# Gated values of the first chunk begun in an earlier memory unit, their casts one step later, residual rows loaded two blocks ahead

## The chip, the cores and the metric

The kernel runs on one core of a Trainium2 chip. A core has TensorE (PE in the profile, with its weight loads apart as PEld), VectorE (DVE), ScalarE (ACT), GpSimd (POOL) and SyncE (SP, here the one queue from which every DMA is issued). The metric is the device time of one execution in microseconds; lower is better.

## The reference

One decoder layer on 2048 tokens of width 1024, in fp32. With this depth its mixer is the dilated sliding-window attention; four memory heads attend to 256 memory tokens.

```python
h = rmsnorm(x, norm_g[i])
proj = h @ w_in[i]                       # q | k | v | memory q | gate
mix = dilated_window_mixer(q, k, v)      # 3 groups of 4 heads; groups weighted by their softmax denominators
mo = memory_attention(qm, rmsnorm(mem, mem_norm_g[i]), w_mem_kv[i])
y = jnp.concatenate([mix, mo], axis=-1) * jax.nn.silu(gate)
x = x + y @ w_out[i]
return rmsnorm(x, final_norm_g)
```

## The kernel before, in words

Every fp32 product of the projections is made of three fp32r matrix multiplications: an operand is split into a rounded high part and the rest (xH, xL for the values, wh, wl for the weights), and high x high, low x high and high x low are added up in one PSUM bank (L140 to L142, and L665 to L667 in the output stage).

The work goes in order of units. Six pairs of sequence heads come first, four chunks of 512 tokens each. Then come eight memory units (the loop at L806), each with a query projection, a gate projection and the attention of two memory heads over one chunk. The output stage follows (`out_block`, L650): 16 blocks of 128 tokens, four to a chunk c, each with two banks of 512 columns (three in the last), and each bank with eight values of k times three multiplications, called a chain of 24 here. There are three PSUM banks of this kind, so a chain can begin when the bank of the chain three earlier has been read. The reader is the residual addition (L670), which adds the row of x to the bank; a square sum, a root and a scaling with g_fin follow, and the row is stored (L687).

A unit's attention has parts that drag on behind it. Score steps (L451 on PE) fill banks; ACT takes the exponentials (L460) into one of four buffers p; POOL divides by the sums (L467); DVE transposes 32 x 32 blocks (L329), SP stores them to a DRAM buffer t_dr (L332) and loads them back turned (L338); a value step (L440, eight small multiplications for one half of a unit) then reads that p. Two halves fill one bank, and DVE multiplies it by the gate u (L420, the gate product). A p buffer is given to a new softmax when the value step that read it is done. The nine value steps from 773.69 us on are numbered 1 to 9 in what follows.

A gated value (`make_y`, L617) of chunk c and index k (128 of the 1024 columns, as many as one k of a chain needs) goes back from DRAM: z_dr holds the gated product and f_dr the group weights of the sequence heads. SP issues z and, for k below 6, two loads of f; after two steps z and f are multiplied (the weighing or product, L634, on POOL for k of 1 and 4, on DVE else); after three ACT casts the high part (L635); after four DVE makes the rest (L636). Four buffers for z and three for f go round.

The program is written with delays: `at(d, fn)` puts fn d steps later, and a step is a part of a projection or of a block; a unit and a block have eight steps. A scheduler then sets each engine's order of instructions from dependences and its own cost estimates. At run time every engine takes its instructions strictly in that order, and so does SP with the DMAs: an instruction that waits holds up those behind it.

The lines that the change touches: `make_y` and its staging buffers (L615 to L636), the loading of a residual row (L657, called in `out_block`), and the two loops that place these steps (L811 to L815, and L822 to L824).

Of the kernel before, what the change touches and what calls it, by code (L numbers as in the profile page):

```python
# [9 lines left out]
F32 = mybir.dt.float32  # L10
F32R = mybir.dt.float32r
AF = mybir.ActivationFunctionType
ALU = mybir.AluOpType
# [4 lines left out]
P = 128  # L18
# [3 lines left out]
CH = 512  # L22
# [12 lines left out]
def trunk_kernel(ctx, tc, xT, xrows, w_in, g_in, w_out, memT, mrows, g_mem, w_mem, g_fin, nbias, ident_in, out):  # L35
    nc = tc.nc
    v, a, pe, gp, sp = nc.vector, nc.scalar, nc.tensor, nc.gpsimd, nc.sync
# [9 lines left out]
    Rb = const.tile([P, S], F32, name="Rb")  # L47
# [19 lines left out]
    def sb(shape, dt, tag, bufs):  # L67
        return pool.tile(shape, dt, tag=tag, name=f"{tag}_{nc.next_id()}", bufs=bufs)
# [4 lines left out]
    def pbank(p=ps_p, tag="pp"):  # L73
        return p.tile([P, CH], F32, tag=tag, name=f"{tag}_{nc.next_id()}")
# [32 lines left out]
    def r_view(g, c):  # L107
        if g == 0:
            return Rb.rearrange("p (r c n) -> p r c n", r=16, c=4)[:, :, c, :]
        if g == 1:  # L110
            return Rb.rearrange("p (j r n) -> p j r n", j=4, r=4)[:, :, c, :]
        return Rb[:, c * CH:(c + 1) * CH]
# [31 lines left out]
    def proj_mm(ps, w, g, c):  # L144
        for k in range(NK):
            proj_k_mm(ps, w, g, c, k)
            if k % 2 and k < NK - 1:
                yield
# [98 lines left out]
    def scaled(dst, ps, g, c):  # L247

        v.tensor_tensor(to_blocks(dst, g), from_proj(ps, g), r_blocks(g, c), op=ALU.mult)  # L249
# [32 lines left out]
    def proj_q(st, g, c, w, ps=None):  # L282
        if ps is None:
            ps = pbank()
            yield from proj_mm(ps, w, g, c)
        q = sb([P, CH], F32, "q", 2)
        if g == 3:
            v.scalar_tensor_tensor(q, ps, SCALE, r_view(g, c), op0=ALU.mult, op1=ALU.mult)
        else:
            scaled(q, ps, g, c)  # L290
        st["q"] = q
        yield
# [322 lines left out]
    staged = []  # L615

    def make_y(c, k):  # L617

        yH, yL = xH[:, 2 + c % 2, k, :], xL[:, 2 + c % 2, k, :]
        cs = slice(c * CH, (c + 1) * CH)  # L620
        if not staged:
            kk = sb([P, 5 * P], F32, "kk", 2)
            vb = sb([P, 5, P], F32, "vb", 2).rearrange("p b n -> p (b n)")
            staged.append([Rb[:, i * CH:(i + 1) * CH] for i in range(3)] + [vb[:, :CH]])
            staged.append([sb([P, CH], F32, "wraw", 2), sb([P, CH], F32, "wraw", 2), kk[:, :CH]])
        t, f = staged[0][k % 4], staged[1][k % 3]
        sp.dma_start(t, z_dr[k // 2][:, k % 2, cs])
        if k < 6:
            for h in range(2):
                sp.dma_start(f[h * HD:(h + 1) * HD, :],  # L630
                             f_dr[k // 2, 2 * (k % 2) + h:2 * (k % 2) + h + 1, cs].broadcast_to([HD, CH]))

        if k < 6:
            at(2, lambda: (gp if k in (1, 4) else v).tensor_tensor(t, t, f, op=ALU.mult))  # L634
        at(3, lambda: a.copy(yH, t))  # L635
        at(4, lambda: v.tensor_tensor(yL, t, yH.bitcast(F32), op=ALU.subtract))  # L636

    outr = out.rearrange("(u r) d -> r u d", r=16)
    gfin = []
# [2 lines left out]
    def load_rows(r):  # L642
        residual[r] = row_tile("wh")
        sp.dma_start(residual[r], xr[r])
# [5 lines left out]
    def out_block(c, b):  # L650
        yH, yL = xH[:, 2 + c % 2], xL[:, 2 + c % 2]
        r = 4 * c + b
        bs = slice(b * P, (b + 1) * P)
        x_t = residual.pop(r)
        last = r == 15
        if not last:
            at(3, lambda: load_rows(r + 1))  # L657
        cuts = (0, 512, 768, 1024) if last else (0, 512, 1024)
        ss = sb([P, 6], F32, "ss", 2)
        sq = row_tile("wl")  # L660
        for i, (lo, hi) in enumerate(zip(cuts, cuts[1:])):
            ns = slice(lo, hi)
            ps = pbank()[:, :hi - lo]
            for k in range(NK):
                pe.matmul(ps, yH[:, k, bs], woH[:, k, ns], start=(k == 0), stop=False)  # L665
                pe.matmul(ps, yH[:, k, bs], woL[:, k, ns], start=False, stop=False)  # L666
                pe.matmul(ps, yL[:, k, bs], woH[:, k, ns], start=False, stop=(k == NK - 1))  # L667
                if k % 2:
                    yield
            v.tensor_tensor(x_t[:, ns], ps, x_t[:, ns], op=ALU.add)  # L670
            if last:
                a.activation(sq[:, ns], x_t[:, ns], AF.Square, accum_out=ss[:, 3 + i:4 + i])
                if i == 0:
                    v.tensor_tensor(x_t[:, ns], x_t[:, ns], gfin[0][:, ns], op=ALU.mult)
        if last:
            v.tensor_reduce(ss[:, 0:1], ss[:, 3:6], axis=AX.X, op=ALU.add)
        else:
            a.activation(sq, x_t, AF.Square, accum_out=ss[:, 0:1])
        rsqrt_mean(ss[:, 1:2], ss[:, 0:1], ss[:, 2:3], ss[:, 3:4])
        if last:  # L680
            a.activation(x_t[:, :CH], x_t[:, :CH], AF.Copy, scale=ss[:, 1:2])
            v.scalar_tensor_tensor(x_t[:, CH:], x_t[:, CH:], ss[:, 1:2], gfin[0][:, CH:], op0=ALU.mult, op1=ALU.mult)
            for n in range(2):
                sp.dma_start(outr[r][:, n * CH:(n + 1) * CH], x_t[:, n * CH:(n + 1) * CH])
        else:
            v.scalar_tensor_tensor(x_t, x_t, ss[:, 1:2], gfin[0], op0=ALU.mult, op1=ALU.mult)
            at(2, lambda: sp.dma_start(outr[r], x_t))  # L687
# [11 lines left out]
    def at(delay, fn):  # L699
        todo.setdefault(slot[0] + delay, []).append(fn)  # L700

    def run(gen):
        for _ in gen:
            for fn in todo.pop(slot[0], []):
                fn()
            slot[0] += 1
# [39 lines left out]
    for idx, (g, pp) in enumerate(pairs):  # L746
# [21 lines left out]
        if idx < 5:  # L768
            n = 2 * pairs[idx + 1][0] + pairs[idx + 1][1]
# [36 lines left out]
    for n, (pp, c) in enumerate(((0, 0), (0, 1), (1, 0), (1, 1), (0, 2), (1, 2), (0, 3), (1, 3))):  # L806
        st = {}
        if n == 3:
            for i in range(2 * NK):
                at(4 * i // 3, lambda i=i: load_wo(i))  # L810
        elif n == 6:  # L811
            for k in range(NK):
                at(2 * k, lambda k=k: make_y(0, k))
        elif n == 7:
            at(3, lambda: load_rows(0))  # L815
            at(5, load_gfin)
        run(proj_q(st, 3, c, ws[2 + 2 * pp]))
        run(proj_gate(st, 3, c, ws[1 + 2 * pp], "nb" if n % 3 == 1 else "u"))
        burst((st, 3, pp, c), 2)
    for c in range(NC):  # L820
        for b in range(4):
            if c < NC - 1:  # L822
                for i in range(2):
                    at(1 + 3 * i, lambda k=2 * b + i: make_y(c + 1, k))  # L824
            run(out_block(c, b))
            if c == 0 and b in (0, 2):
                burst()
# [62 lines left out]
```

## Time and profile before

| | |
|---|---|
| median of 3 runs | 999.66 us (999.1 to 1000.13) |
| profiled execution | 999.68 us |
| its span | 997.6 us |
| PE busy | 964.0 us (97%) |
| DVE busy | 428.0 us (43%) |
| ACT busy | 325.6 us (33%) |
| POOL busy | 244.3 us (24%) |
| mean granted clock of TensorE | 0.982 |

The span runs from the first to the last instruction of the profiled execution. PEclk, the granted clock, is a share of 2.4 GHz. A row of the timeline gives the start in us from the span's start, how long the instruction took, the engine, the line, the operation, output and inputs, and in brackets the idle time of the engine before it and what ended that. Matmul rows overlap: the time from one start to the next is what one costs. Line numbers are those of the kernel before; in the changed kernel the same code stands two or three lines further down (weighing L636, cast L637, rest L638, row load L646, chains L667 to L669, residual addition L672, store L689).

### The profile page before, as it was taken

The page shows a single profiled execution, that of the slowest core. Times are in us where ns is not written, and L with a number is a line of the kernel's source. Part 1 is how long each engine was busy: PE and PEld are TensorE (multiplying, and loading weights), DVE is VectorE, ACT ScalarE, POOL GpSimd, SP SyncE. Part 2 cuts the span into 40 slices and gives each one's busy share as a digit, 9 for nine tenths or more (in the row PEclk, how much of TensorE's full clock was granted, in tenths as well). Part 3 has the DMA queues.
Part 4 walks back from the last instruction along what each step waited for, and adds up shares of the span by engine and source line. Part 5 has one row for each costly group of instructions (what it writes and reads, how often), then busy time and mean ns, then how long its engine had stood idle before and what let it go on. Part 6 is the DMA issues. An engine that isn't in the chain of part 4 may idle for free.

```text
span 997.6 us, 13866 instructions
## 1 busy us (share of the span) xinstructions
PE 964.0 (97%) x4836; PEld 757.9 (76%) x4836; DVE 428.0 (43%) x995; ACT 325.6 (33%) x992; POOL 244.3 (24%) x391
## 2 busy tenths in 40 slices
PE   8899999999999999999999999999999788999997
PEld 5688888887788887877777777787777466788886
DVE  7867333333333333333334334335543544465333
ACT  5756432242223222332233232433232330232111
POOL 4411500050004100321123011245356450011000
PEclk9899999999999999999999999999999889899999
DMA  5455321141224322442345432534465876877311
GB/s 196 156 190 190 127 75 53 54 144 67 76 86 133 124 82 85 129 136 85 95 117 157 121 92 85 174 134 129 117 213 172 219 224 182 272 242 234 127 64 63
DMA packets 102133, 135.17 MB, mean 136 GB/s; under 512 B 29872, under 2 KB 63920, under 8 KB 102064
## 3 DMA queue, kind: packets, MB, share of 16 engines
q1 hardware_dynamic: 102064, 134.30, 42.9%
q8 instruction: 38, 0.62, 0.3%
q14 instruction: 31, 0.25, 0.1%
HBM read 89.14 MB, written 45.12 MB: 135 GB/s over the span
## 4 chain that ended last, share of the span: by engine, by line
PE 86%; DMA 3%; DVE 3%; issue 3%; POOL 2%; ACT 1%; SPq 1%; POOLq 0%; ACTq 0%; DVEq 0%
PE pp L140 20%; PE pp L142 19%; PE pp L141 19%; PE pp L665 6%; PE pp L666 6%; PE pp L667 6%; PE ps L395 4%; PE po L417 3%; PE ps L451 1%; PE po L440 1%; DMA wraw<-in_w_in 1%; POOL p L467 1%; POOL wl L78 1%; DMA wl<-in_g_fin 1%; DMA wh<-in_xrows 1%
## 5 line engine op out<-in xcount | busy, mean ns | idle before, releaser
L140 PE MATMUL pp<-xH,wh 128*128 128x512 f32 x896 | 360.9, 403 | 3.0 <-DVE kk L249 2.9
L142 PE MATMUL pp<-xH,wl 128*128 128x512 f32 x896 | 356.9, 398 | 1.8 <-DVE wl L78 1.8
L141 PE MATMUL pp<-xL,wh 128*128 128x512 f32 x896 | 356.9, 398 | 1.4 <-DVE xL L198 1.4
L140 PEld LDWEIGHTS pp<-xH,wh 128*128 128x128 f32 x896 | 169.5, 189 | 51.6 <-issue 7.7
L142 PEld LDWEIGHTS pp<-xH,wl 128*128 128x128 f32 x896 | 169.2, 189 | 46.0 <-DVE wl L78 3.6
L141 PEld LDWEIGHTS pp<-xL,wh 128*128 128x128 f32 x896 | 169.5, 189 | 42.8 <-DVE xL L198 2.7
L320 POOL COPY vb<-mid 32x128 f32<-32x128 f32 (+1 forms) x208 | 59.4, 285 | 248.5 <-DVE mid L317 240.3
L665 PE MATMUL pp<-xH 128*128 128x512 f32 (+1 forms) x264 | 105.3, 399 | 12.0 <-ACT xH L635 6.6
L320 ACT COPY vb<-mid 32x128 f32<-32x128 f32 (+1 forms) x208 | 60.7, 292 | 167.4 <-DVE mid L317 165.3
L666 PE MATMUL pp<-xL,xH 128*128 128x512 f32 (+1 forms) x264 | 104.2, 395 | 0.0
L667 PE MATMUL pp<-xH,xL 128*128 128x512 f32 (+1 forms) x264 | 103.2, 394 | 0.8 <-DVE xL L636 0.7
L78 POOL TENSOR_TENSOR wl<-wraw,wh 128x512 fp32r<-128x512 f32 x52 | 67.1, 1303 | 144.1 <-ACT wh L77 138.2
L374 ACT ACTIVATE p<-p,nm_all 128x128 f32<-128x128 f32 (+1 forms) x192 | 86.1, 450 | 43.3 <-DVE nm_all L373 27.6
L329 DVE STREAM_TRANSPOSE mid<-p 128x1024 f32<-128x1024 f32 (+1 forms) x56 | 66.9, 1194 | 52.6 <-DMA t_dr<-mid 35.2
L467 POOL TENSOR_SCALAR p<-p,sm 128x256 f32<-128x256 f32 x64 | 63.2, 1005 | 71.9 <-DVE sm L463 55.2
L306 DVE SCALAR_TENSOR_TENSOR tmp<-pp,Rb 128x512 f32<-128x512 f32 x32 | 22.1, 691 | 123.8 <-PE pp L142 123.7
L665 PEld LDWEIGHTS pp<-xH 128*128 128x128 f32 x264 | 51.4, 195 | 25.8 <-ACT xH L635 8.6
L307 ACT ACTIVATE u<-tmp 128x512 f32<-128x512 f32 x29 | 18.3, 630 | 139.8 <-DVE tmp L306 138.7
L667 PEld LDWEIGHTS pp<-xH,xL 128*128 128x128 f32 x264 | 51.2, 194 | 12.9 <-DVE xL L636 2.2
L373 DVE CUSTOM_DVE_ANT_0 p<-ps,nb 128x128 f32<-128x128 f32 (+1 forms) x192 | 57.1, 362 | 7.8 <-PE ps L395 7.7
L666 PEld LDWEIGHTS pp<-xL,xH 128*128 128x128 f32 x264 | 51.5, 195 | 10.4 <-issue 0.4
L249 DVE TENSOR_TENSOR q<-pp,Rb 128x512 f32<-128x512 f32 x24 | 16.5, 689 | 81.8 <-PE pp L142 81.8
(130 smaller groups left out, 822.2 us busy)
## 6 DMA issues: line engine op xcount, KB each, us to landing
t_dr<-mid SPq DMA_DIRECT2D x46, 512.0 KB, 3.0
p<-t_dr SPq DMA_DIRECT2D x184, 128.0 KB, 3.4
wraw<-in_w_in SPq DMA_DIRECT2D x56, 256.0 KB, 2.9
wh<-in_xrows SPq DMA_DIRECT2D x16, 512.0 KB, 5.5
out<-wh SPq DMA_DIRECT2D x15, 512.0 KB, 3.1
z_dr<-u SPq DMA_DIRECT2D x29, 256.0 KB, 3.0
Rb<-z_dr SPq DMA_DIRECT2D x24, 256.0 KB, 5.6
tmp<-in_xT SPq DMA_DIRECT2D x22, 256.0 KB, 3.7
```

Of the source, the lines that this page charges most:

```text
L78: on.tensor_tensor(wl, raw, wh.bitcast(F32), op=ALU.subtract)
L140: pe.matmul(ps, wh[:, k, :], xh, start=(k == 0), stop=False)
L141: pe.matmul(ps, wh[:, k, :], xl, start=False, stop=False)
L142: pe.matmul(ps, wl[:, k, :], xh, start=False, stop=(k == NK - 1))
L320: (gp.tensor_copy if (i + j) % 2 else a.copy)(dst[32 * j:32 * j + 32, :, 32 * i:32 * i + 32], mid[32 * i:32 * i + 32, :, 32 * j:32 * j + 32])
L329: v.transpose(mid.rearrange("p (j t b) -> p t j b", j=4, t=n), src.rearrange("p (t j b) -> p t j b", t=n, j=4))
L373: v.tensor_tensor_reduce(p, sc, bias, -SCALE, BIG, ALU.add, ALU.min, nm)
L374: a.activation(p, p, AF.Exp, bias=nm, scale=-1.0, accum_out=l)
L467: gp.tensor_scalar(w, w, sm[:, 1, h, b:b + 1], None, op0=ALU.mult)
L665: pe.matmul(ps, yH[:, k, bs], woH[:, k, ns], start=(k == 0), stop=False)
L666: pe.matmul(ps, yH[:, k, bs], woL[:, k, ns], start=False, stop=False)
L667: pe.matmul(ps, yL[:, k, bs], woH[:, k, ns], start=False, stop=(k == NK - 1))
```

## The change

Three things differ. The gated values of chunk 0 begin in the sixth memory unit (n = 5, from its fourth step on) and not at the start of the seventh. Cast and rest come four and five steps after the loads and not three and four, and in chunks 1 to 3 the loads of a pair are placed at steps 0 and 3 of a block and not at 1 and 4. A residual row is loaded two blocks before its use and not one. The staging buffers change places to fit the earlier start: k of 0 takes the second quarter of Rb and the f buffer in kk, and the two wraw buffers are taken when k of 1 and 2 ask for them.

```diff
--- before.py
+++ after.py
@@ -621,8 +621,10 @@
         if not staged:
             kk = sb([P, 5 * P], F32, "kk", 2)
             vb = sb([P, 5, P], F32, "vb", 2).rearrange("p b n -> p (b n)")
-            staged.append([Rb[:, i * CH:(i + 1) * CH] for i in range(3)] + [vb[:, :CH]])
-            staged.append([sb([P, CH], F32, "wraw", 2), sb([P, CH], F32, "wraw", 2), kk[:, :CH]])
+            staged.append([Rb[:, CH:2 * CH], vb[:, :CH], Rb[:, 2 * CH:3 * CH], Rb[:, :CH]])
+            staged.append([kk[:, :CH]])
+        elif len(staged[1]) < 3:
+            staged[1].append(sb([P, CH], F32, "wraw", 2))
         t, f = staged[0][k % 4], staged[1][k % 3]
         sp.dma_start(t, z_dr[k // 2][:, k % 2, cs])
         if k < 6:
@@ -632,8 +634,8 @@
 
         if k < 6:
             at(2, lambda: (gp if k in (1, 4) else v).tensor_tensor(t, t, f, op=ALU.mult))
-        at(3, lambda: a.copy(yH, t))
-        at(4, lambda: v.tensor_tensor(yL, t, yH.bitcast(F32), op=ALU.subtract))
+        at(4, lambda: a.copy(yH, t))
+        at(5, lambda: v.tensor_tensor(yL, t, yH.bitcast(F32), op=ALU.subtract))
 
     outr = out.rearrange("(u r) d -> r u d", r=16)
     gfin = []
@@ -653,8 +655,8 @@
         bs = slice(b * P, (b + 1) * P)
         x_t = residual.pop(r)
         last = r == 15
-        if not last:
-            at(3, lambda: load_rows(r + 1))
+        if r < 14:
+            at(3, lambda: load_rows(r + 2))
         cuts = (0, 512, 768, 1024) if last else (0, 512, 1024)
         ss = sb([P, 6], F32, "ss", 2)
         sq = row_tile("wl")
@@ -808,12 +810,13 @@
         if n == 3:
             for i in range(2 * NK):
                 at(4 * i // 3, lambda i=i: load_wo(i))
-        elif n == 6:
+        elif n == 5:
             for k in range(NK):
-                at(2 * k, lambda k=k: make_y(0, k))
+                at(4 + 2 * k, lambda k=k: make_y(0, k))
         elif n == 7:
             at(3, lambda: load_rows(0))
             at(5, load_gfin)
+            at(7, lambda: load_rows(1))
         run(proj_q(st, 3, c, ws[2 + 2 * pp]))
         run(proj_gate(st, 3, c, ws[1 + 2 * pp], "nb" if n % 3 == 1 else "u"))
         burst((st, 3, pp, c), 2)
@@ -821,7 +824,7 @@
         for b in range(4):
             if c < NC - 1:
                 for i in range(2):
-                    at(1 + 3 * i, lambda k=2 * b + i: make_y(c + 1, k))
+                    at(3 * i, lambda k=2 * b + i: make_y(c + 1, k))
             run(out_block(c, b))
             if c == 0 and b in (0, 2):
                 burst()
```

The order of the instructions moves in these places.

PE, where the last projection ends, in the kernel before (value step 1 is po_6870, ps are score banks, pp_7256, pp_7301 and pp_7366 the first three chains, all with k = 0):

```order
L440 MATMUL po_6870<-p_6594,vb_6068 64x256 x4
L451 MATMUL ps_7068<-kk_5788,q_6976 128x256 x2
L451 MATMUL ps_7070<-kk_5788,q_6976 128x256 x2
L665 MATMUL pp_7256<-xH 128x512
L666 MATMUL pp_7256<-xL,xH 128x512
L665 MATMUL pp_7301<-xH 128x512
L667 MATMUL pp_7256<-xH,xL 128x512
L666 MATMUL pp_7301<-xL,xH 128x512
L667 MATMUL pp_7301<-xH,xL 128x512
```

and in the changed kernel, where pp_7262, pp_7307 and pp_7369 are these chains and po_6883 is value step 1:

```order
L667 MATMUL pp_7262<-xH 128x512
L668 MATMUL pp_7262<-xL,xH 128x512
L669 MATMUL pp_7262<-xH,xL 128x512
L667 MATMUL pp_7307<-xH 128x512
L668 MATMUL pp_7307<-xL,xH 128x512
L669 MATMUL pp_7307<-xH,xL 128x512
L667 MATMUL pp_7369<-xH 128x512
L668 MATMUL pp_7369<-xL,xH 128x512
L669 MATMUL pp_7369<-xH,xL 128x512
L440 MATMUL po_6883<-p_6594,vb_6068 64x256 x4
L451 MATMUL ps_7079<-kk_5788,q_6987 128x256 x2
L451 MATMUL ps_7081<-kk_5788,q_6987 128x256 x2
```

The nine multiplications of k = 0 went ahead of value step 1 and of the score step behind it. Before, value step 2 and then k = 1 come next; now k = 1 and 2 come next, and then value step 2.

POOL at the same place, before (L467 normalises a half, L634 is the weighing of k = 1; that of k = 4 is the next row):

```order
L467 TENSOR_SCALAR p_6889<-p_6889,sm_6891 128x2x128 x4
L467 TENSOR_SCALAR p_6912<-p_6912,sm_6914 128x2x128 x4
L634 TENSOR_TENSOR Rb<-Rb,wraw_6941 128x512
L467 TENSOR_SCALAR p_7053<-p_7053,sm_7055 128x2x128 x4
L467 TENSOR_SCALAR p_7076<-p_7076,sm_7078 128x2x128 x4
```

and in the changed kernel (L636 is the weighing):

```order
L467 TENSOR_SCALAR p_6902<-p_6902,sm_6904 128x2x128 x4
L467 TENSOR_SCALAR p_6925<-p_6925,sm_6927 128x2x128 x4
L636 TENSOR_TENSOR vb_6835<-vb_6835,wraw_6864 128x512
L467 TENSOR_SCALAR p_7064<-p_7064,sm_7066 128x2x128 x4
L636 TENSOR_TENSOR Rb<-Rb,wraw_6864 128x512
```

The weighing of k = 1 stays behind the normalising of the same half; the weighing of k = 4 now stands behind one half less.

DVE behind value step 5 before (po_7195 is its bank, wh the row of the residual addition):

```order
L420 TENSOR_TENSOR u_6821<-u_6821,po_7195 128x512
L329 STREAM_TRANSPOSE mid_7285<-p_7076 128x8x4x32
L670 TENSOR_TENSOR wh_7139<-pp_7256,wh_7139 128x512
L463 RECIPROCAL sm_7239<-sm_7239 128x4
L634 TENSOR_TENSOR Rb<-Rb,wraw_6939 128x512
L670 TENSOR_TENSOR wh_7139<-pp_7301,wh_7139 128x512
```

and in the changed kernel (po_7201), where on PE the chain pp_7502 comes directly behind value step 5 and takes the bank of pp_7369:

```order
L420 TENSOR_TENSOR u_6821<-u_6821,po_7201 128x512
L329 STREAM_TRANSPOSE mid_7289<-p_7087 128x8x4x32
L463 RECIPROCAL sm_7245<-sm_7245 128x4
L672 TENSOR_TENSOR wh_7197<-pp_7369,wh_7197 128x512
L672 TENSOR_TENSOR wh_7197<-pp_7416,wh_7197 128x512
L636 TENSOR_TENSOR Rb<-Rb,kk_6833 128x512
```

Now the first residual addition behind the gate product is that of the second block (wh_7197), and a reciprocal stands in front of it.

PE at value step 8 before (po_7537; pp_7552 and pp_7585 are the two chains of the last block of chunk 0):

```order
L667 MATMUL pp_7552<-xH,xL 128x512
L440 MATMUL po_7537<-p_7214,vb_6068 64x256 x4
L665 MATMUL pp_7585<-xH 128x512
L666 MATMUL pp_7585<-xL,xH 128x512
L667 MATMUL pp_7585<-xH,xL 128x512
```

and in the changed kernel (po_7540; pp_7631 and pp_7670 are the first two chains of chunk 1, here with k = 3):

```order
L440 MATMUL po_7540<-p_7220,vb_6068 64x256 x4
L667 MATMUL pp_7631<-xH 128x512
L668 MATMUL pp_7631<-xL,xH 128x512
L669 MATMUL pp_7631<-xH,xL 128x512
L667 MATMUL pp_7670<-xH 128x512
L668 MATMUL pp_7670<-xL,xH 128x512
L669 MATMUL pp_7670<-xH,xL 128x512
```

Value steps 7 and 8 moved from the last block of chunk 0 into the first chain of chunk 1. Before, 16 multiplications stand between the two, and the whole of pp_7585 and three values of k between step 8 and k = 3. Now five stand between them, and k = 3 follows step 8.

SP behind the transposition that follows value step 7, before (mid is the transposed half, wh_7405 the row of block 2, the next z_dr and f_dr rows are k = 3 of chunk 1):

```order
L332 DMA t_dr_85<-mid_7394 128x1024
L687 DMA out<-wh_7139 128x1024
L644 DMA wh_7405<-in_xrows 128x1024
L432 DMA z_dr_81<-u_6980 128x512
L627 DMA vb_6937<-z_dr_79 128x512
L630 DMA wraw_6939<-f_dr 64x512 x2
L338 DMA p_7237<-t_dr_85 32x4x256 x4
```

and in the changed kernel (wh_7412 is the row of block 3):

```order
L332 DMA t_dr_85<-mid_7397 128x1024
L689 DMA out<-wh_7146 128x1024
L629 DMA Rb<-z_dr_79 128x512
L632 DMA kk_6833<-f_dr 64x512 x2
L646 DMA wh_7412<-in_xrows 128x1024
L432 DMA z_dr_81<-u_6991 128x512
L338 DMA p_7243<-t_dr_85 32x4x256 x4
```

The row of block 2 no longer stands there; its load is ahead of this store now. The loads of k = 3 of chunk 1 stayed, and the row of block 3 stands where that of block 2 was.

## Rows read from the trace of the kernel before

**Rows 1.** the page's part 1: busy us, share of the span, instructions

```profile
PE 964.0 (97%) x4836; PEld 757.9 (76%) x4836; DVE 428.0 (43%) x995; ACT 325.6 (33%) x992; POOL 244.3 (24%) x391
```

**Rows 2.** waits of TensorE over the span: us, times, longest

```profile
PE pp L665 <- ACT xH L635: 6.6, 3, 3.6
PE pp L665 <- DVE wh L670: 5.3, 2, 5.1
```

**Rows 3.** two stretches, each with its length, busy us of engines, clock, DMA

```profile
773.69:875.61 101.92, 85.88 (x361) 62.04 (x361) 49.42 (x83) 26.39 (x69) 30.51 (x29) 0.88 0.76 226
875.61:990.39 114.78, 114.72 (x529) 95.82 (x527) 51.83 (x100) 21.73 (x39) 10.66 (x15) 1.00 0.45 147
```

**Rows 4.** timeline of TensorE: start, us, instruction, idle time before it

```profile
773.69 1.08 PE L440 MATMUL po<-p,vb 128*64 128x256 f32 x8
776.40 1.58 PE L451 MATMUL ps<-kk,q 64*128 64x256 f32 x8 [1.63 <-ACT p L460]
...
784.62 0.55 PE L665 MATMUL pp<-xH 128*128 128x512 f32 x1 [1.75 <-ACT xH L635]
...
794.84 2.52 PE L451 MATMUL ps<-kk,q 64*128 64x256 f32 x8 [1.63 <-ACT p L460]
...
809.18 0.79 PE L665 MATMUL pp<-xH 128*128 128x512 f32 x1 [3.57 <-ACT xH L635]
...
818.50 0.50 PE L665 MATMUL pp<-xH 128*128 128x512 f32 x1 [0.23 <-DVE wh L670]
...
849.23 0.80 PE L665 MATMUL pp<-xH 128*128 128x512 f32 x1 [5.10 <-DVE wh L670]
...
853.22 0.39 PE L665 MATMUL pp<-xH 128*128 128x512 f32 x1
```

**Rows 5.** timeline of DVE, ACT and POOL, 773 to 785

```profile
773.80 0.69 DVE L306 SCALAR_TENSOR_TENSOR tmp<-pp,Rb 128x512 f32<-128x512 f32 x1 [3.66 <-PE pp L142]
...
774.87 0.47 ACT L460 ACTIVATE p<-ps,sm 128x256 f32<-128x256 f32 x1 [6.63 <-DMA p<-t_dr]
...
776.59 0.65 DVE L634 TENSOR_TENSOR Rb<-Rb,wraw 128x512 f32<-128x512 f32 x1
...
777.42 4.03 POOL L467 TENSOR_SCALAR p<-p,sm 128x256 f32<-128x256 f32 x4 [4.22 <-DVE sm L463]
...
781.42 1.27 POOL L634 TENSOR_TENSOR Rb<-Rb,wraw 128x512 f32<-128x512 f32 x1
...
783.96 0.61 ACT L635 CAST xH<-Rb 128x512 fp32r<-128x512 f32 x1
```

**Rows 6.** timeline of POOL, 800 to 820

```profile
808.02 5.46 POOL L467 TENSOR_SCALAR p<-p,sm 128x256 f32<-128x256 f32 x4 [6.66 <-issue]
```

**Rows 7.** timeline behind a value step, 838 to 849

```profile
838.14 1.08 PE L440 MATMUL po<-p,vb 128*64 128x256 f32 x8
...
839.27 0.69 DVE L420 TENSOR_TENSOR u<-u,po 128x512 f32<-128x512 f32 x1 [5.83 <-PE po L440]
...
839.88 1.24 DVE L329 STREAM_TRANSPOSE mid<-p 128x1024 f32<-128x1024 f32 x1
...
841.14 0.34 SPq L332 DMA_DIRECT2D t_dr<-mid  x1
...
842.00 0.73 SPq L644 DMA_DIRECT2D wh<-in_xrows  x1
...
848.48 1.29 DVE L670 TENSOR_TENSOR wh<-pp,wh 128x512 f32<-128x512 f32 x2 [5.41 <-DMA wh<-in_xrows]
```

**Rows 8.** waits of SP's queue, 745 to 998

```profile
SPq L332 <- DVE mid L329: 19.5, 4, 9.3
```

**Rows 9.** timeline of SP and POOL, 849 to 858

```profile
850.43 1.09 SPq L630 DMA_DIRECT2D wraw<-f_dr  x2
...
856.69 1.29 POOL L634 TENSOR_TENSOR Rb<-Rb,wraw 128x512 f32<-128x512 f32 x1 [4.81 <-DMA wraw<-f_dr]
```

**Rows 10.** the page's part 6: issues, KB each, us to landing

```profile
wraw<-in_w_in SPq DMA_DIRECT2D x56, 256.0 KB, 2.9
```

## The prediction

> **What bounds the kernel now.** The page's first part is read first: TensorE is busy 97% of the span [rows 1], so a change can give only what TensorE loses. The waits of TensorE say where: the two longest, 11.9 us together, are at L665, the first multiplication of the output stage, for the cast of a gated value (ACT L635, 6.6) and for a residual addition (DVE L670, 5.3) [rows 2]. A table of two stretches shows that they lie together: from 773.69, where the last projection ends, to 875.61 TensorE is busy for 85.88 of 101.92 us at a granted clock of 0.88; from there to 990.39 it is busy for 114.72 of 114.78 us at 1.00 [rows 3]. So the first stretch is the account, and 875.61 is my mark: 11 chains of 24 multiplications, nine value steps (L440) and three score steps (L451) lie between, before and after the change alike.
>
> The timeline of TensorE in that stretch gives the longest stops: 1.63 twice for score steps, 1.75 and 3.57 for casts, 5.10 for a residual addition [rows 4]. After each of them the clock is at 1.2 GHz for a while: 0.43 us between starts of multiplications where 0.23 is usual at 2.4 GHz; from 849.23 nine of them take 3.99 us [rows 4]. Work at full clock is 264 x 0.23 + 9 x 1.1 + 3 x 1.25 = 74.4 us (1.1 and 1.25 are estimates from starts in the timeline); idle time is 16.0; the remaining 11.5 of 101.9 us are the slow clock (0.12 x 101.9 = 12.2 says the same).
>
> **The change part by part.** No instruction is added or dropped; what counts is the order on in-order queues. I walk the new order from 773.69 with the durations of this trace: softmax of a half 1.85 us on ACT (four of 0.47 with their sums), normalising it on POOL 4.03, a product 0.65 on DVE or 1.27 on POOL, a cast 0.61, a rest as long as a product [rows 5]. The buffers' new order costs nothing: the first weight half and both wraw buffers, which the output weights still use, are now needed from k=1 on, when these have been split.
>
> *Begin in the sixth unit.* The loads of k=0 are issued near 763 and its product stands on DVE where this was idle for 3.66 us ahead of 773.80 [rows 5]; the cast is done by 771.5. So the nine multiplications of k=0 run from 773.69 to 775.8 at full clock; before, they stood behind value step 1 and ran at half clock. That gains 9 x 0.195 = 1.75 us. The price: value step 1 ends at 776.9 instead of 774.8, and all that hangs on it moves by 2.1 us: softmax at 776.95, score step 1.53 later as now (774.87 to 776.40), so at 778.5 after the same idle time, normalising from 779.0 to 783.05. Behind this normalising POOL's queue holds the product of k=1, as before: 784.3, and its cast 784.95. TensorE has done all that it may do by 780.1 and waits 4.9 us, from then on at half clock. Before, the same chain (softmax 774.87, POOL 777.42 and 781.42, cast 783.96) let TensorE go on at 784.62, with one value step more behind it [rows 4, 5]. After this round the change is behind by 0.4 + 1.1 us.
>
> *Casts one step later.* k=1 and k=2 now run together: 785.0 to 791.1 (nine at 0.43, nine at 0.23); value step 2 to 792.2; a score step from 793.8, slow, to 795.8 (1.55 idle); k=3 at 796.95 (1.15 idle), k=4 at 800.85, value step 3 to 804.05; the last score step from 805.7 (1.65 idle) to 807.3. k=5 to 7 follow without a wait, since their casts stand right behind the softmax; three chains are complete at 815.25 and nine multiplications more at 817.35. Before, these were complete at 818.1, with one value step more [rows 4]: the change is 0.4 us behind, although the stop of 3.57 is gone.
>
> POOL's normalising ahead of k=4 I take at 4.5 us; its bounds are 4.03 [rows 5] and 5.46 [rows 6]. The Trainium skill (SBUF — State Buffer, SBUF: two separate sides) says that a DVE instruction with two SBUF inputs and a POOL instruction that reads SBUF exclude each other for their whole length. Two such DVE instructions, the product and the rest of k=3, would fall beside it; by that rule it would take 4.03 + 1.3 = 5.3 and the sum would be 0.8 us longer, which my range holds. The 5.46, beside which DVE ran such instructions, agrees with it.
>
> *A bank behind value step 5.* In the new order a chain of multiplications follows value step 5 directly (pp_7502 in the order rows). Its bank comes free with a residual addition, and on DVE this stands behind the gate product, the transposition and a reciprocal, which wait for this value step and the softmax after it. From the step's end at 828.6: softmax 1.95, reciprocal 0.15, addition 0.65, so TensorE restarts at 831.35 after 2.75 us of idle time, with nine multiplications at half clock (1.8). Before, multiplications that needed no bank came next, and the only wait for an addition there is 0.23 us [rows 4]. Cost 4.5.
>
> *Rows two blocks ahead.* Row 2 is issued near 832 and needed at 840: the stop of 5.10 us at 849.23 goes, with 1.8 us of slow clock. What made that stop decides the rest. SP stood for the transposition behind value step 7: the step at 838.14, gate product 839.27, transposition 839.88, its store 841.14, then the row at 842.00, landed at 848.48 [rows 7]; SP's longest wait of this kind is 9.3 us [rows 8]. This wait stays, and in the new order the loads of k=3 of chunk 1 and of row 3 stand behind it. I come to 851.95 for value step 7. From its end at 852.95: gate product and transposition 1.9, then k=2's product and cast, done at 856.15; TensorE has two multiplications left meanwhile and waits 2.75. The store goes at 854.9; the loads of k=3 are issued until 857.3 and land 5.2 later (a POOL product waited until 856.69 for loads issued until 851.5 [rows 9]), 862.5; product and cast 863.8. TensorE has three multiplications and value step 8 in between and waits 5.2. Before, 49 multiplications (11.2 us) stood between value step 7 and k=3 and hid this. The bounds of the landing are 2.9, the median of the weight loads [rows 10], and 6.5, the row's [rows 7]; I stay at 5.2, the same loads at the same place.
>
> From there the second chain starts near 865.2, with row 3; value step 9 is done at 872.6, and 36 multiplications more reach my mark at 881.7, 6.1 later. By sums: 74.4 of work, idle 1.55 + 4.9 + 1.55 + 1.15 + 1.65 + 2.75 + 2.75 + 5.2 + 0.6 = 22.1, slow clock 12: 108.5 against 101.9, 6.6 later. Behind the mark nothing is late: no transpositions are left on SP. The profiled execution took 999.68 us (span 997.6 and 2.1 around it), the median of the three runs is 999.66. So 999.7 + 6 = 1005.7, rounded to 1005.5.
>
> **Rivals.** *Faster.* The new stops don't form, because value steps 5 and 7 come early enough for DVE, and only the gains are left: 5.1 + 1.8 less the 0.4 behind gives 993.2 us. For it speaks that TensorE's longest stop is a late row, which the change mends; against it the order of DVE and SP, which no earlier load alters. The Trainium skill (Trainium Kernel Development and Optimization, Best Practices) advises to double-buffer so that loads overlap compute, and by this the rival would come true; the 9.3 us that SP stood are a wait for a transposition, which a further buffer doesn't shorten [rows 8].
>
> *No change.* Only one of the two late stops forms: 993.2 + 4.5 to 8 = 998 to 1001.
>
> *Slower still.* Chunks 2 and 3 start with casts that are one step later too, and TensorE waits for them at each start: twice 1.6 us and 1.2 of slow clock, 1011 us. Against it: DVE is busy for only 51.83 of the 114.78 us behind the mark [rows 3].
>
> **How the numbers follow.** Stops as walked 0.52, slower still 0.08, no change 0.15, faster 0.25. What a measurement here can tell from no change is 0.2%, 2 us. So slower 0.60, same 0.15, faster 0.25. The likeliest case's own range is 1001 to 1010: the landing gives -2.3 and +1.3, POOL -0.5 and +1, the slow clock 1.5 either way. The range of 8 in 10 takes in no change and most of faster: 993 to 1010.
>
> **What would show it.** In the new profile: nine multiplications of k=0 ahead of a value step at 775.8; a stop of 4 to 5 us before k=1, for POOL's product through ACT; no long wait for a row; a stop of 2.5 to 3 us for a residual addition behind value step 5; two stops, near 3 and 5 us, for casts at the start of chunk 1; the mark 6 us later. I am wrong if k=1's cast comes before 783, or if TensorE runs through value steps 5 and 7 without a stop.

## The result

The changed kernel takes 1007.33 us (median of 6 runs, 1003.78 to 1008.28) against 999.52 for the kernel before on the same chip: a ratio of 1.0078 with a 95% interval of [1.0067, 1.0090]. The forecast was 1005.5, slower. The profiled execution took 1006.83 us, its span is 1004.6, 7.0 more than before.

The waits of TensorE over the span (us in total, times, longest), against [rows 2]:

```profile
PE pp L667 <- ACT xH L637: 15.3, 4, 6.3
...
PE pp L667 <- DVE wh L672: 2.9, 1, 2.9
```

The wait for a residual addition has shrunk from 5.3 to 2.9, the one for a cast has more than doubled, from 6.6 to 15.3.

Two stretches of the new profile, from the end of the last projection to the mark, and from there to the end of TensorE's work (columns as in [rows 3]: busy us of PE, PEld, DVE, ACT, POOL, clock, DMA):

```profile
773.31:882.47 109.16, 86.11 (x361) 62.58 (x359) 46.66 (x78) 23.98 (x65) 28.17 (x29) 0.87 0.65 204
882.47:997.30 114.83, 114.83 (x529) 95.93 (x528) 53.60 (x103) 23.38 (x42) 11.95 (x15) 1.00 0.47 151
```

The whole loss lies ahead of the mark: 109.16 us against 101.92 for the same work [rows 3]. Behind it the time is the same (114.83 against 114.78). 109.16 - 86.11 = 23.05 us are idle; with 74.4 us of work at full clock, 11.7 are left for the slow clock.

The timeline of TensorE there, its value steps and stops, against [rows 4]:

```profile
775.36 1.08 PE L440 MATMUL po<-p,vb 128*64 128x256 f32 x8
778.07 1.58 PE L451 MATMUL ps<-kk,q 64*128 64x256 f32 x8 [1.63 <-ACT p L460]
784.33 0.79 PE L667 MATMUL pp<-xH 128*128 128x512 f32 x1 [4.67 <-ACT xH L637]
...
797.55 0.79 PE L667 MATMUL pp<-xH 128*128 128x512 f32 x1 [1.81 <-ACT xH L637]
...
827.59 1.08 PE L440 MATMUL po<-p,vb 128*64 128x256 f32 x8
831.55 0.79 PE L667 MATMUL pp<-xH 128*128 128x512 f32 x1 [2.87 <-DVE wh L672]
...
851.75 1.08 PE L440 MATMUL po<-p,vb 128*64 128x256 f32 x8
856.00 0.50 PE L667 MATMUL pp<-xH 128*128 128x512 f32 x1 [2.50 <-ACT xH L637]
857.15 1.08 PE L440 MATMUL po<-p,vb 128*64 128x256 f32 x8
...
864.54 0.79 PE L667 MATMUL pp<-xH 128*128 128x512 f32 x1 [6.31 <-ACT xH L637]
...
872.47 1.08 PE L440 MATMUL po<-p,vb 128*64 128x256 f32 x8
```

The stops of 5.10 and 3.57 us have gone, and four stand in their place: 4.67 for k=1 (1.75 before), 2.87 for a bank, 2.50 and 6.31 for k=2 and k=3 of chunk 1. Three of these four can be followed back.

The first, in the timelines of POOL and ACT, against [rows 5]:

```profile
778.78 3.62 POOL L467 TENSOR_SCALAR p<-p,sm 128x256 f32<-128x256 f32 x4 [5.34 <-DMA p<-t_dr]
782.37 1.26 POOL L636 TENSOR_TENSOR vb<-vb,wraw 128x512 f32<-128x512 f32 x1
783.66 0.62 ACT L637 CAST xH<-vb 128x512 fp32r<-128x512 f32 x1 [5.18 <-POOL vb L636]
```

POOL's product stands behind four normalisations and ACT waits 5.18 us for it.

The second, in the timeline of DVE behind value step 5:

```profile
828.73 0.69 DVE L420 TENSOR_TENSOR u<-u,po 128x512 f32<-128x512 f32 x1 [6.32 <-PE po L440]
829.33 1.24 DVE L329 STREAM_TRANSPOSE mid<-p 128x1024 f32<-128x1024 f32 x1
830.74 0.18 DVE L463 RECIPROCAL sm<-sm 128x4 f32<-128x4 f32 x1 [0.17 <-ACT p L460]
830.83 1.26 DVE L672 TENSOR_TENSOR wh<-pp,wh 128x512 f32<-128x512 f32 x2
```

The addition that frees the bank comes behind the gate product, a transposition and a reciprocal.

The fourth, in the timelines of DVE, SP and ACT behind value step 7, against [rows 7, 9]:

```profile
852.88 0.69 DVE L420 TENSOR_TENSOR u<-u,po 128x512 f32<-128x512 f32 x1 [6.99 <-PE po L440]
853.48 1.24 DVE L329 STREAM_TRANSPOSE mid<-p 128x1024 f32<-128x1024 f32 x1
...
854.75 0.34 SPq L332 DMA_DIRECT2D t_dr<-mid  x1
...
856.37 1.82 SPq L632 DMA_DIRECT2D kk<-f_dr  x2
...
863.15 0.69 DVE L636 TENSOR_TENSOR Rb<-Rb,kk 128x512 f32<-128x512 f32 x1 [6.48 <-DMA kk<-f_dr]
863.87 0.62 ACT L637 CAST xH<-Rb 128x512 fp32r<-128x512 f32 x1 [7.93 <-DVE Rb L636]
```

SP's queue stands for the transposition that stands for the value step, and the loads of k=3 are behind it. Both were so before; what is new is that TensorE has only five multiplications left meanwhile.

### The profile page after: what moved, and what is told of

It is laid out like the page before. It is cut to its first block, busy times and chain, and to the rows that moved or that the text cites. A ratio compares the mean times of both kernels' runs of the same rounds, so it can differ in the third digit from the quotient of the medians.

```text
span 1004.6 us, 13871 instructions
## 1 busy us (share of the span) xinstructions
PE 963.4 (96%) x4836; PEld 757.8 (75%) x4836; DVE 428.0 (43%) x995; ACT 325.2 (32%) x992; POOL 244.9 (24%) x391
## 5 line engine op out<-in xcount | busy, mean ns | idle before, releaser
L667 PE MATMUL pp<-xH 128*128 128x512 f32 (+1 forms) x264 | 106.6, 404 | 18.2 <-ACT xH L637 15.3
L467 POOL TENSOR_SCALAR p<-p,sm 128x256 f32<-128x256 f32 x64 | 60.9, 970 | 82.2 <-DVE sm L463 53.9
L306 DVE SCALAR_TENSOR_TENSOR tmp<-pp,Rb 128x512 f32<-128x512 f32 x32 | 22.1, 691 | 120.9 <-PE pp L142 120.8
L249 DVE TENSOR_TENSOR tmp<-pp,Rb 128x512 f32<-128x512 f32 x24 | 16.6, 691 | 82.8 <-PE pp L142 82.7
```

The costliest lines, as they stand in the source:

```text
L467: gp.tensor_scalar(w, w, sm[:, 1, h, b:b + 1], None, op0=ALU.mult)
```

## The experiments

Ratios are to the kernel before, run on the same chip beside each experiment. "Changed" is the changed kernel with an edit, "before" the kernel before with one.

| run | edit | median us | ratio, interval |
|---|---|---|---|
| e1 | changed, k=1's product on DVE | 1003.13 | 1.0033 [1.0020, 1.0047] |
| e2 | changed, k=3 of chunk 1 two steps earlier | 1004.30 | 1.0043 [1.0029, 1.0056] |
| e3 | before, rows two blocks ahead | 993.87 | 0.9944 [0.9930, 0.9957] |
| e4 | before, first chunk begun early | 1009.11 | 1.0093 [1.0080, 1.0106] |
| e5 | changed, another bank for one chain | 999.52 | 1.0002 [0.9992, 1.0012] |
| e6 | changed, four links mended | 998.80 | 0.9999 [0.9990, 1.0007] |
| e7 | before, casts one step later | 999.71 | 1.0001 [0.9992, 1.0011] |
| e8 | e3 with k=1 on DVE, k=5 a step earlier | 994.51 | 0.9955 [0.9937, 0.9972] |
| e9 | changed, bank of e5 and k=1 of e1 | 996.63 | 0.9971 [0.9959, 0.9983] |
| e10 | changed, pairs at steps 1 and 4 again | 1006.47 | 1.0072 [1.0056, 1.0088] |
| e11 | e8 again | 993.41 | 0.9957 [0.9930, 0.9983] |

**e3, e4 and e7: the parts alone.**

```diff
# e3, on the kernel before
-        if not last:
-            at(3, lambda: load_rows(r + 1))
+        if r < 14:
+            at(3, lambda: load_rows(r + 2))
...
             at(5, load_gfin)
+            at(7, lambda: load_rows(1))
# e4, on the kernel before, with the staging buffers of the change
-        elif n == 6:
+        elif n == 5:
             for k in range(NK):
-                at(2 * k, lambda k=k: make_y(0, k))
+                at(4 + 2 * k, lambda k=k: make_y(0, k))
# e7, on the kernel before
-        at(3, lambda: a.copy(yH, t))
-        at(4, lambda: v.tensor_tensor(yL, t, yH.bitcast(F32), op=ALU.subtract))
+        at(4, lambda: a.copy(yH, t))
+        at(5, lambda: v.tensor_tensor(yL, t, yH.bitcast(F32), op=ALU.subtract))
```

> The kernel before with the rows loaded two blocks ahead and nothing else of the change. Theory: the stop of 5.10 us for row 2 goes with its 1.8 us of slow clock, value step 7 comes near 839.6, k=3 of the second chunk is loaded by 852.3 and needed near 853.3, k=4 makes a stop of about 0.8: 993.5 us (991 to 997). So the gain of the rows is there when the rest of the change isn't. Rival (SP's wait for the transposition makes k=3 late here too, a stop of some 5 us in place of the row's): 998 to 1000.

> The kernel before with the first chunk begun in the sixth unit and the staging buffers that this needs; casts, rows and the pairs of the later chunks stay as before. Theory: the order up to value step 5 is that of the changed kernel, so the stop of 4 to 5 us ahead of k=1 is there; value step 6 follows value step 5 directly, and the residual addition stands on DVE behind a transposition that waits for POOL's normalising, so TensorE waits some 7 us near 830 to 837. The second chunk starts late enough for its loads, so no stop for k=3. In sum about 1001 us (999 to 1004). Rival (the early begin carries the whole loss): 1006 to 1008.

> The kernel before with casts and rests one step later and nothing else of the change. Theory: the scheduler's order hardly moves (value step 7 comes three multiplications earlier, the rest of one k stands behind a transposition), no link of the chain of stops is new, row 2 is as late as before: 999 us, within 0.2% of before (997.5 to 1001). Rival (a cast one step later reaches TensorE later at each of eight values of k, three with a wait of 0.6 us): 1001.5 to 1003.

The rows alone gain 5.6 us, as expected to within 0.4. In their profile TensorE waits for no row; what it waits for (columns as above), and its stop for k=3 of chunk 1, are

```profile
PE pp L665 <- ACT xH L635: 9.1, 5, 3.6
...
PE pp L665 <- DVE wh L670: 0.2, 1, 0.2
```

```profile
854.44 0.50 PE L665 MATMUL pp<-xH 128*128 128x512 f32 x1 [1.45 <-ACT xH L635]
```

The wait for the addition is down from 5.3 to 0.2, and k=3 makes a stop of 1.45 us only. Row 3 now stands behind the transposition's store and holds DVE's addition for 4.83 us, but TensorE has other work meanwhile. The later casts alone change nothing; in the changed kernel, delays of three and four steps even give every engine the same order, instruction for instruction.

The early begin alone costs 9.6 us, more than the whole change; the rival was right, though 1009 lies above its range, and my 1001 was wrong. Its profile shows why, in the timelines of SP, DVE and PE:

```profile
831.87 0.34 SPq L332 DMA_DIRECT2D t_dr<-mid  x1
832.25 0.43 SPq L646 DMA_DIRECT2D wh<-in_xrows  x1
...
834.91 1.25 DVE L329 STREAM_TRANSPOSE mid<-p 128x1024 f32<-128x1024 f32 x1 [0.72 <-DMA t_dr<-mid]
837.25 1.29 DVE L672 TENSOR_TENSOR wh<-pp,wh 128x512 f32<-128x512 f32 x2 [1.10 <-DMA wh<-in_xrows]
...
838.00 0.79 PE L667 MATMUL pp<-xH 128*128 128x512 f32 x1 [6.13 <-DVE wh L672]
...
860.42 0.80 PE L667 MATMUL pp<-xH 128*128 128x512 f32 x1 [6.72 <-DVE wh L672]
```

I had expected the first of these stops for DVE's order, and that is the larger part of it: the addition stands behind a transposition that ends at 836.16, 4.3 us after TensorE has stopped (838.00 - 6.13 = 831.87). That transposition waited for a store to land, not for POOL's normalising, and row 1, issued at 832.25 behind a transposition's store, then held the addition for 1.10 us more. I had left out the second stop: row 2 is late as before (6.72 against 5.10). So in this kernel additions wait for two late rows and not one. The two parts don't add: -5.6 and +9.6 would give 1003.5, and the change takes 1007.3. Loading two blocks ahead takes both row stops away, and the bank and the two casts at the start of chunk 1 take their place.

**e1: k=1's product.**

```diff
-            at(2, lambda: (gp if k in (1, 4) else v).tensor_tensor(t, t, f, op=ALU.mult))
+            at(2, lambda: (gp if (c, k) != (0, 1) and k in (1, 4) else v).tensor_tensor(t, t, f, op=ALU.mult))
```

> The changed kernel with one edit: the product of k=1 of the first chunk is on DVE and not on POOL, where it stood behind the normalising. Nothing else moves in the order of any engine. Theory (the stop of 4.67 us ahead of k=1 is POOL's queue: normalising 778.78 to 782.40, product to 783.6, cast to 784.3): DVE makes the product right after the first of two reductions, near 779.9 to 780.6, the cast ends at 781.2, TensorE goes on at 781.3, the stop is 1.6 us. 3 us earlier from there, and no other stop grows: about 1004.3 us (1003 to 1005.5). Rival (the stop is covered by what comes next, score step and k=3 wait the longer): no change, 1007.

The stop at k=1 is 1.74 us and not 4.67, and the stops that follow come 2.1 to 2.5 us earlier with their lengths changed by 0.3 at most:

```profile
781.86 0.80 PE L667 MATMUL pp<-xH 128*128 128x512 f32 x1 [1.74 <-ACT xH L637]
```

POOL's queue behind the normalising was the cause. The profiled executions differ by 2.45 us, the medians by 4.2, where 3 were expected; no trace shows what the medians gain beyond the stop.

**e2: the loads of k=3.**

```diff
-                    at(3 * i, lambda k=2 * b + i: make_y(c + 1, k))
+                    at(1 if (c, b, i) == (0, 1, 1) else 3 * i, lambda k=2 * b + i: make_y(c + 1, k))
```

> The changed kernel with one edit: k=3 of the second chunk is begun two steps earlier in its block, so its loads stand on SP ahead of the transposition's store behind value step 7, not behind it. Theory (the stop of 6.31 us at 864.54 is SP waiting for that transposition until 854.75, with the loads of k=3 behind it): the loads go out near 845, the product stands on DVE right behind that of k=2, near 856, and the stop of 6.3 us is gone; k=4, whose loads come later on SP, then makes one of 1 to 2 us. About 4.5 us gained: 1002.8 us (1000.5 to 1004.5). Rival (k=3 is late because of DVE or the cast, not of its loads): the stop stays, 1007.

The stop of 6.31 us for k=3 is gone, so it was its loads, and the time is 1004.3 where 1002.8 was expected. But the next late thing was not k=4: it was row 3, whose load still stands behind the transposition's store. In the timelines of SP, DVE and PE:

```profile
851.21 0.34 SPq L332 DMA_DIRECT2D t_dr<-mid  x1
...
852.07 0.73 SPq L646 DMA_DIRECT2D wh<-in_xrows  x1
...
859.76 1.29 DVE L672 TENSOR_TENSOR wh<-pp,wh 128x512 f32<-128x512 f32 x2 [4.65 <-DMA wh<-in_xrows]
...
860.51 0.79 PE L667 MATMUL pp<-xH 128*128 128x512 f32 x1 [3.72 <-DVE wh L672]
```

**e5 and e9: the bank.**

```diff
# e5
-            ps = pbank()[:, :hi - lo]
+            ps = (pbank(ps_s, "ps") if (r, i) == (2, 1) else pbank())[:, :hi - lo]
# e9: the same and the edit of e1
```

> The changed kernel with one edit: the second chain of block 2 (the first that follows value step 5 directly) takes a bank of the score steps, which are through by then, so it needs no residual addition before it. Theory (the stop of 2.87 us at 831.55 is the bank, which a residual addition behind the gate product, the transposition and a reciprocal frees): the stop and its 1.8 us of slow clock go, the value steps behind it come earlier by as much, and the stops at the start of the second chunk keep their length since they hang on value step 7: about 1003 us (1001 to 1005.5). Rival (the chains ahead of the second chunk hold TensorE only until its loads come, so the later stops grow by as much): 1006.5 to 1007.5.

> The changed kernel with the other bank for the second chain of block 2 and k=1's product of the first chunk on DVE; loads of k=3 and of the rows as the change has them. Theory (the four edits mended together gave back what these two gain, because the row and the loads of k=3 stood ahead of a transposition's store and delayed it): 999.5 - 3 to 4 = 996 us (994.5 to 997.5). Rival (whatever is gained at k=1 is lost at the second chunk, so that the kernel stays where the bank alone brought it): 999 to 1000.

One bank gives back the whole loss of the change. The stop of 2.87 us is gone, and the one for k=3 is 2.95 and not 6.31. I had expected the second to stay, and 999.5 is below my range. The profile of e5 shows what moved, in the timelines of DVE, SP and PE:

```profile
847.21 1.24 DVE L329 STREAM_TRANSPOSE mid<-p 128x1024 f32<-128x1024 f32 x1
849.45 0.69 DVE L420 TENSOR_TENSOR u<-u,po 128x512 f32<-128x512 f32 x1 [1.00 <-PE po L440]
...
848.47 0.34 SPq L332 DMA_DIRECT2D t_dr<-mid  x1
...
850.10 1.83 SPq L632 DMA_DIRECT2D kk<-f_dr  x2
...
857.90 0.51 PE L667 MATMUL pp<-xH 128*128 128x512 f32 x1 [2.95 <-ACT xH L637]
```

The scheduler puts the transposition ahead of the gate product of value step 7, so its store no longer waits for that step, and the loads of k=3 go out at 850.10 instead of 856.37. How much of the 7.8 us is the bank itself and how much this second move, e5 does not separate; the stops fell by 2.87 + 0.46 and by 3.36 - 0.48. With k=1 on DVE as well the ratio falls by another 0.3% (996.6 us, expected 996), where e1 alone had lowered it by 0.45%: within the intervals these two prices add up.

**e6: four links at once.**

```diff
# the edits of e1, e2 and e5, and
-            at(3, lambda: load_rows(r + 2))
+            at(1, lambda: load_rows(r + 2))
```

> The changed kernel with the four late links mended together: k=1's product of the first chunk on DVE, the other bank for the chain behind value step 5, k=3 of the second chunk begun two steps earlier, and the rows loaded in step 1 of a block instead of step 3, so that no row stands behind a transposition's store. Theory (these links are the whole loss, and their prices add up): stops of 2.95, 2.87 and 6.31 us go and two or three stretches of slow clock of some 1.8 us with them, 1007.3 - 12.1 - 1.8 to 5.4 = 990 to 993.5, so about 992 us (989 to 996), at least as fast as the rows alone. Rival (TensorE has too little work between the value steps when the first chunk is begun early, so that other stops take their place): 998 to 1002.

This was wrong: 998.8 and not 992. The stops named are gone, but k=4 of chunk 1 makes one of 3.99 us. Waits of SP's queue from 840 to 866 (first row), and the timelines of SP, POOL and PE:

```profile
SPq L338 <- DMA t_dr<-mid: 5.3, 2, 4.7
```

```profile
844.95 0.58 SPq L646 DMA_DIRECT2D wh<-in_xrows  x1
845.64 0.38 SPq L332 DMA_DIRECT2D t_dr<-mid  x1
...
852.29 2.53 SPq L338 DMA_DIRECT2D p<-t_dr  x4
...
855.34 1.09 SPq L632 DMA_DIRECT2D wraw<-f_dr  x2
...
861.66 1.26 POOL L636 TENSOR_TENSOR Rb<-Rb,wraw 128x512 f32<-128x512 f32 x1 [6.11 <-DMA wraw<-f_dr]
...
863.62 0.80 PE L667 MATMUL pp<-xH 128*128 128x512 f32 x1 [3.99 <-ACT xH L637]
```

The row and the loads of k=3 now go out just ahead of the transposition's store; the load of p that needs this store starts 6.65 us after it, SP stands 4.7 us for that, and the loads of k=4 stand behind. So the rival's time came, and another stop took the place of those mended: row 3 in e2, k=4 here. e9, without the edits on SP's order, is 0.3% faster, and the intervals don't meet. Little of that is a stop: up to the mark the idle time is 14.1 us in e9 and 14.6 in e6. By the sum used above the slow clock makes the difference, 10.5 against 12.4 us.

**e10: the pairs of the later chunks.**

```diff
-                    at(3 * i, lambda k=2 * b + i: make_y(c + 1, k))
+                    at(1 + 3 * i, lambda k=2 * b + i: make_y(c + 1, k))
```

> The changed kernel with one part undone: the later chunks' pairs of k are begun at steps 1 and 4 of a block again, as before the change, not at 0 and 3. Theory: the order up to value step 5 is the same, the chain behind it waits for its bank as long, and the loads of k=3 then stand behind the row too, behind the same transposition, so that stop is 0.5 to 2 us longer: 1008 us (1006.5 to 1010). Rival (the earlier pairs are what made k=3 late): 1000 to 1003.

No change from the changed kernel (the intervals overlap), against both: the stop for k=3 is 1.27 and not longer, while row 3 makes one of 2.87 and k=2 one of 3.17. Here too, casts of three and four steps give the same order, so this run is the early begin and the rows together: the later pairs are no part of the loss.

**e8 and e11: a candidate beyond both.**

```diff
# on e3
-            at(2, lambda: (gp if k in (1, 4) else v).tensor_tensor(t, t, f, op=ALU.mult))
+            at(2, lambda: (gp if k in ((4,) if c == 0 else (1, 4)) else v).tensor_tensor(t, t, f, op=ALU.mult))
...
-                at(2 * k, lambda k=k: make_y(0, k))
+                at((0, 2, 4, 6, 8, 9, 12, 14)[k], lambda k=k: make_y(0, k))
```

> A candidate beyond both: the kernel before with the rows two blocks ahead, k=1's product of the first chunk on DVE, and k=5 begun one step earlier, so that its cast stands on ACT ahead of the four exponentials that wait for value step 4, not behind them. Theory: of the stop of 3.57 us at 807.91 some 2 us go, since nine multiplications more lie ahead of value step 4 and k=6 becomes the late one; k=1 saves up to 1.5 us: 993.9 - 2 to 3.5, so about 991 us (989.5 to 993). Rival (loads of k=5 ahead of the p loads of value step 4 on SP make that step late by as much): 993.5 to 994.5.

> The candidate of before (rows two blocks ahead, k=1's product on DVE, k=5 a step earlier) once more, since its executions lay between 990.2 and 997.7 us while its stops add up to less than with the rows alone. Theory (TensorE's clock, not a stop, makes the difference: in the profile of 997.4 us the granted clock was 0.66 from 784 to 794, where the rows alone had 1.00): a profiled execution near 991 us shows the same stops within 0.2 us each and a clock of 0.9 or more in that stretch; one near 997 shows 0.66 again. Rival (a transfer is late in some executions): the stops differ by several us, the clock doesn't.

In both profiles the stop of 3.57 us at k=5 has gone and one of 2.59 stands at k=6, the idle time up to the mark is 12.0 and 11.8 us against 12.8 with the rows alone, and the time is the same within the intervals. From 784 to 794, with the columns of [rows 3], e3 and e8 read:

```profile
784.00:794.00 10.00, 7.87 (x38) 5.10 (x40) 6.21 (x10) 4.44 (x15) 4.01 (x4) 1.00 0.93 234
```

```profile
784.00:794.00 10.00, 8.33 (x21) 5.39 (x22) 3.85 (x7) 3.59 (x11) 3.68 (x4) 0.66 0.83 233
```

and e11 has a clock of 0.56 there. From value step 2 to value step 3 all three do the same work, one score step and 18 multiplications, with one stop of 1.70 to 1.75 us: it takes 8.95 us in e3, 12.55 in e8 and 14.17 in e11. Both profiled executions of the candidate took longer than its median (spans 995.7 and 996.1), so no profile shows this stretch in one near 991 us. But the mean granted clock of every execution is on record: in e8 and e11 together the twelve of at most 994.1 us had 0.987 to 0.991, and of the nine longer ones, 995.2 to 1002.6 us, seven had 0.980 to 0.984 and two 0.987. So the spread goes with the clock, as the theory said; what sets the clock in one execution and not in another stays open. No kernel measured is faster by its ratio than the one with the rows alone, 0.6% faster than before.

## Why the prediction was right

The direction, the size and the chain of stops were right; what was assigned to which part of the change was not. By its own steps:

- *Begin in the sixth unit.* The nine multiplications of k=0 end where value step 1 starts, at 775.36 (predicted 775.8), the stop ahead of k=1 is 4.67 (4.9), TensorE goes on at 784.33 (785.0). e1 shows its cause.
- *Casts one step later.* k=1 and k=2 do run together, but not by this edit, which is worth nothing alone (e7) and changes no order beside the others. It comes from the early begin, so the step was right by luck. The stop for k=3 was 1.81 (1.15): the score step ahead of it took 1.58 and not 2.0, and its product on DVE took 0.92 and not 0.65 beside the normalising.
- *POOL ahead of k=4.* 4.08 us, taken at 4.5. The 4.03 that it was built on held a delay already: four normalisations with no two-input DVE instruction beside them took 3.62, at 778.78. In the 4.08 the last of the four took 1.38 us and not 0.92, beside the rest of k=3. The Trainium skill's rule (SBUF — State Buffer, SBUF: two separate sides) is borne out in part: POOL and DVE did hold each other up, but not for their whole length. By the rule, 3.62 and two DVE instructions of 0.65 would be 4.9, and the 5.46 of [rows 6], beside which DVE ran five such instructions, would be 7.0; both are estimates, and the prediction's 5.3 started from the 4.03.
- *A bank behind value step 5.* 2.87 (2.75), restart at 831.55 (831.35).
- *Rows two blocks ahead.* No row is waited for. Value step 7 stands at 851.75 (851.95), the stops for k=2 and k=3 are 2.50 (2.75) and 6.31 (5.2), value step 9 ends at 873.5 (872.6), the mark is at 882.47 (881.7). The size that was off is the issue of the loads of k=3: it lasted until 858.2 and not 857.3, since two of them took 1.82 us. They landed near 863.1, 4.9 us later (5.2).
- *The sum.* Idle 23.05 (22.1), slow clock 11.7 (12), in all 109.16 (108.5). The last term of the idle sum, 0.6, has no stop to it: the eight stops measured make up the 23.05. The profiled executions differ by 7.15 us, the medians by 7.8, where 6 were forecast.

What failed is the account by parts. The early begin was priced at 0.4 + 1.1 us and the bank and the late casts were put down to other headings; e4 shows that the early begin carries all of the loss, and e3 that the rows by themselves gain 5.6 us with no new stop above 1.45. That "in the new order the loads of k=3 of chunk 1 and of row 3 stand behind" SP's wait is true of the loads of k=3 in both orders, and of row 3 in e3 too. What differs is how much work TensorE still has at value step 7; the prediction counted it (49 multiplications before) under the rows, but it is the early begin that uses it up. Chunk 0 has 192 multiplications. Counted from the timelines, so many multiplications of the output stage were done when each value step came:

| kernel | at value step 5 | 6 | 7 | 8 | 9 |
|---|---|---|---|---|---|
| before | 63 | 100 | 152 | 168 | 204 |
| rows alone (e3) | 63 | 100 | 160 | 201 | 228 |
| early begin alone (e4) | 120 | 120 | 159 | 168 | 204 |
| changed | 120 | 156 | 196 | 201 | 226 |
| changed, other bank (e5) | 123 | 171 | 198 | 201 | 226 |

In e3 50 multiplications lie between value step 7 and k=3 of chunk 1 (the stop of 1.45), in the changed kernel five. Little work left is not enough by itself: in e5 there is as little at value step 7, but the loads of k=3 no longer hang on that step, and the stop is 2.95. And the work can run out elsewhere: in e4 nothing is left between value steps 5 and 6, ahead of the stop of 6.13, while value step 7 comes as early as before. The runs show the cause of the single stops (e1, e2 and, with the second move, e5) and the part that brings them (e3, e4). That the work left is what joins them fits these counts, but no run changes it alone, so that much is argued.

Of the rivals, "faster" is what the rows alone do: 993.9 measured, 993.2 worked out; it failed here because of the early begin, not because further buffers don't help. The advice of the Trainium skill (Trainium Kernel Development and Optimization, Best Practices) to double-buffer, which I had set aside, agrees with e3: the load of row 2 stopped being late once it was issued a block earlier.

## What to carry to other kernels

Filling an engine earlier from a fixed store of independent work doesn't shorten a chain that hangs on another engine; it uses up the work that would have hidden the chain's later links, so count what is left to do at each of them. When an in-order DMA queue holds a store that waits for a computation, look at every load behind it, and ask of each edit which load comes next in that queue. Measure the parts of a change alone: here one part gained 0.6% and another lost 0.9% under one heading.

## What the runs showed of the hardware

- A DVE instruction with two SBUF inputs and a two-input POOL product ran one after the other: in the changed kernel a reciprocal root's multiplication (L155) took 1.14 us at 868.75, where its like take 0.16, and ended with POOL's product from 868.59 to 869.88; POOL's product at 837.26 took 2.03 us instead of 1.27 beside DVE's scaling of a row. With the normalisations, of 0.92 us each, the hold was shorter: of the four that take 4.08 from 794.93 the last, at 797.63, took 1.38 beside the rest of k=3 (797.53 to 798.22), and the product of k=3, from 795.93, took 0.92, although POOL had a normalisation running until 796.75.

```profile
868.59 1.29 POOL L636 TENSOR_TENSOR Rb<-Rb,wraw 128x512 f32<-128x512 f32 x1
...
868.75 1.14 DVE L155 TENSOR_TENSOR ss<-ss 128x1 f32<-128x1 f32 x1
...
794.93 4.08 POOL L467 TENSOR_SCALAR p<-p,sm 128x256 f32<-128x256 f32 x4 [11.30 <-issue]
```

- A store issued right behind large loads landed late: in e6 the load that needs the transposition's store of 845.64 starts 6.65 us after it, and of that line's 56 stores the longest took 6.6 us to land and the median one 2.9.
- Less idle time did not make the kernel faster where the clock stayed low: from 784 to 794 the granted clock was 0.66 and 0.56 in e8 and e11, where it was 1.00 in e3, with TensorE idle for 1.75 us ahead of 784.50 in e3 and for 1.7 us ahead of 785.0 to 785.7 in the other two.
